# Another order for the beginning of a one-core kernel: wider modulation reads, first tokens earlier, gate weights in pairs

## The chip, the cores and the metric

The kernel runs on one core of a Trainium2 chip. The metric is the device time of one execution in microseconds (us); the median of three runs is compared. The engines go by the names of the profile: PE is TensorE's matmul (PEld its weight load), DVE is VectorE, ACT is ScalarE, POOL is GpSimd, and SP is SyncE, which issues most of the transfers (DMAs). Each engine works through its own queue in order, and an instruction that waits holds up all that stands behind it in that queue.

## What is computed

One layer of a flow-matching backbone for 2048 sample tokens and 128 prompt tokens of width 1024. Only the start of it matters here:

```python
def ada_mod(cvec, w, b):
    m = jnp.einsum('...d,de->...e', jax.nn.silu(cvec), w) + b
    return jnp.split(m, 3, axis=-1)
...
shift, scale, gate = ada_mod(c, w_ada[l], b_ada[l])
xn = rmsnorm(h, ln_g[l]) * (1.0 + scale[:, None, :]) + shift[:, None, :]
...
proj = jnp.einsum('btd,de->bte', xn, w_in)
qkv, beta, dec, z_a, u_b, v_b, z_b, x_c, z_c, gates = jnp.split(proj, points, axis=-1)
```

So nothing can be projected before shift and scale are known, and these need 2048 of the 3072 columns of `w_ada` (1024 rows, float32, 8.4 MB). The first projection that the kernel makes is `z_a` (512 columns, later put through SiLU and kept in memory as `sz`); then come `qkv` and the rest: a delta-rule mixer, a spatial gate, a Fourier mixer, merge gates and the output projection.

Each projection is made with three float16 matmuls, for activations and weights are both split into a high and a low part (`xh`, `xl`; `hi`, `lo`): hi·xh + hi·xl + lo·xh. Scales that are powers of two keep both in float16's range.

## The kernel before

**Queue order.** The Python program issues instructions engine by engine, and a planner then orders them by a simulated timeline and by priority: an instruction issued later may be put ahead of one issued earlier where the planner thinks that it can start sooner. `tc.high_priority()` raises the priority of what is issued inside it; `tc.issue_after(x)` keeps instructions behind `x`.

**Modulation (lines 396 to 430).** Eight blocks of 256 columns. Each is read in two chunks of four 128-row groups (`ast`, 512 KB each, eight buffers, line 403). In the blocks named in `AD` the second chunk is summed on DVE (`ada_sum`, lines 384 and 386: a column times a scalar for each of the two conditioning vectors, accumulated in `aacc`) and enters PE by one matmul for each vector (`sel`); everything else is a matmul with the two vectors as the stationary operand (line 411). The block's 2x256 result is copied from PSUM (`adr`, line 413) and transposed in two pieces (line 415). Ahead of block 4 (`XB`) the first 512 tokens are read (`xt`, 2 MB, line 393) and a few small parameters (`columns`, lines 360 to 367). After the last block, lines 420 to 430 make shift (`sh`), scale (`ms`) and a bound on the activations, from which their power-of-two scale `sx` is taken.

**Gate projection (lines 433 to 475).** The weights of `z_a` are four blocks of 128 columns (512 KB, two landing buffers `wst`), read by `read_w` (line 195) and converted by `converting`: squares with a sum (line 209), a power-of-two scale from it (`scales`, lines 180 to 188, with a small matmul and DVE operations), the high half on ACT (line 222), the low half on DVE (line 223). The loop over tiles of tokens (`TBS`: four of 512, then the 128 prompt tokens) makes, for each tile: four sums of squares on ACT (`jk`, line 451), `rsqrt` (lines 170 and 171, the power on POOL), a normalization on DVE (line 455); then for each of eight groups of 128 channels four transposes on PE (line 459), the modulation on DVE (`xm`, line 461, three buffers), the high half on ACT (`xh`, line 462) and the low half on POOL (`xl`, line 463); then for each of the four z blocks 24 matmuls (`gemm_T`, line 466), a sigmoid on ACT (line 468), a product on DVE (line 469) and the store (line 471). All matmuls stand in the helper `mm`, line 161.

**Weights further on.** `wlist` is the list of all later weight blocks. `fetch`, `weight_step` and `getw` read them two ahead and convert them in small steps; after the tile loop `ahead(2)` lets the first two qkv weights go. The read of `w_spatial` (line 649) stands in the program after the qkv projection.

Of the kernel before, what the change touches and what calls it, by code (L numbers as in the profile page):

```python
# [11 lines left out]
F16 = mybir.dt.float16  # L12
I32 = mybir.dt.int32
BF16 = mybir.dt.bfloat16
AF = mybir.ActivationFunctionType
# [16 lines left out]
QUOTA = 1.6  # L32
SCAN = 1.3
MT = 0.015
XB = 4
AD = (0, 2, 4, 6)
CQ = 545
FS = 4096.0
TBS = [(0, 512), (512, 512), (1024, 512), (1536, 512), (2048, 128)]
# [72 lines left out]
def hybrid_flow_kernel(ctx: ExitStack, tc: tile.TileContext, x_prompt, x_sample, state_delta, c, c_ctx, ln_g, w_ada,  # L112
# [47 lines left out]
    def mm(out, l, r, start=True, stop=True):  # L160
        PE.matmul(out, l, r, start=start, stop=stop)  # L161

    def mm3(out, l, r):
# [2 lines left out]
        mm(out, l[0], r[1], False, False)  # L166
        mm(out, l[1], r[0], False, True)

    def rsqrt(out, ss, mul, w):
        V.tensor_scalar(out, ss, mul, EPS, ALU.mult, ALU.add)  # L170
        G.tensor_tensor(out, out, mhalf.to_broadcast([P, w]), ALU.pow)  # L171
# [18 lines left out]
    def load_w(src, nkt, cols=P, hi=None, lo=None, tag="w", bufs=5):  # L190
        return convert(read_w(src, nkt, cols, tag), nkt, cols, hi, lo, tag, bufs)

    def read_w(src, nkt, cols=P, tag="w"):
        st = sb(wp, [P, nkt, cols], "wst" if cols == P else tag + "st", bufs=2 if cols == P else 1)
        SY.dma_start(st, src.rearrange("(k p) c -> p k c", p=P))
        return st

    def converting(w, st, nkt, cols=P, hi=None, lo=None, tag="w", bufs=5):

        wpool = bwp[0] if tag == "b" else wp  # L200
        if tag == "z":
            hi, lo = [sb(p0p, [P, nkt, cols], n_, F16, bufs=4) for n_ in ("zhi", "zlo")]
# [6 lines left out]
        A.activation(w.lo, st, AF.Square, accum_out=ss)  # L209
# [12 lines left out]
        A.activation(w.hi, st, AF.Copy, scale=s)  # L222
        V.scalar_tensor_tensor(w.lo, st, s, w.hi, ALU.mult, ALU.subtract)  # L223
# [27 lines left out]
    def xrows(t0, n):  # L251
        return xs_[t0:t0 + n, :] if t0 < NS else xp_[t0 - NS:t0 - NS + n, :]

    wlist = []
    for c0 in [C_ZA + g * P for g in range(4)]:
        wlist.append((w_in_[:, c0:c0 + P], KT, "z", 4))
# [122 lines left out]
    def ada_sum(acc, st, ks, fresh=True):  # L379

        for g in range(2):
            for i, k in enumerate(ks):
                if i == 0 and fresh:
                    V.tensor_scalar(acc[:, g, :], st[:, i, :], scT[:, k, g:g + 1], None, ALU.mult)
                else:
                    V.scalar_tensor_tensor(acc[:, g, :], st[:, i, :], scT[:, k, g:g + 1], acc[:, g, :], ALU.mult, ALU.add)
# [9 lines left out]
    for blk in range(8):  # L396
        if blk == XB:
            load_x(*TBS[0])
            columns()
        ps = bank(ps_d, [2, 256])  # L400
        for k0 in range(0, KT, 4):
            st = sb(p0p, [P, 4, 256], "ast", bufs=8)
            last_ada = SY.dma_start(st, w_ada_[k0 * P:(k0 + 4) * P, blk * 256:(blk + 1) * 256].rearrange("(k p) c -> p k c", p=P))
            if k0 and blk in AD:
                acc = sb(p0p, [P, 2, 256], "aacc")
                ada_sum(acc, st, range(k0, k0 + 4))
                for g in range(2):
                    mm(ps, sel[:, g, :], acc[:, g, :], False, g == 1)
                continue
            for k in range(4):  # L410
                mm(ps, scT[:, k0 + k, :], st[:, k, :], k0 + k == 0, k0 + k == KT - 1)
        adr = sb(p0p, [2, 256], "adr")
        V.tensor_copy(adr, ps)
        for k in range(2):
            PE.transpose(pa[:, blk * 2 + k, :], adr[:, k * P:(k + 1) * P], ident[:2, :2])
    ms = sb(cp, [P, KT, 2], "ms")
    sh = sb(cp, [P, KT, 2], "sh")
    with tc.high_priority():
# [12 lines left out]


    szD = dram("sz", [H, P, NTOK])
    with tc.issue_after(last_ada.ins):
        read_next()
        read_next()
        load_x(*TBS[1])
        zaw = getw(4)
        bdp = sb(wp, [P, KT, 32], "bdp", F16, bufs=1)
        bdw = load_w(w_in_[:, C_BD:C_BD + 16], KT, 16, hi=bdp[:, :, 0:16], lo=bdp[:, :, 16:32], tag="d")  # L440
    szlate = []
    for ti, (t0, tn) in enumerate(TBS):
        if t0 not in xts:
            load_x(t0, tn)
        g = 0 if t0 < NS else 1
        nt = tn // P
        xt = xts[t0]
        jk = sb(p0p, [P, D], "jk", F16, bufs=1)
        xss = sb(p0p, [P, nt], "xss")
        for j in range(nt):  # L450
            A.activation(jk, xt[:, j, :], AF.Square, accum_out=xss[:, j:j + 1])
        rs = sb(p0p, [P, nt], "rs")
        rsqrt(rs, xss, 1.0 / D, nt)
        for j in range(nt):
            V.tensor_scalar(xt[:, j, :], xt[:, j, :], rs[:, j:j + 1], None, ALU.mult)
        for k in range(KT):
            ps = bank(ps_d, [P, tn])
            for j in range(nt):
                PE.transpose(ps[:, j * P:(j + 1) * P], xt[:, j, k * P:(k + 1) * P], ident)
            t = sb(p0p, [P, tn], "xm", bufs=3)  # L460
            V.tensor_scalar(t, ps, ms[:, k, g:g + 1], sh[:, k, g:g + 1], ALU.mult, ALU.add)
            A.copy(xh[:, k, t0:t0 + tn], t)
            G.tensor_tensor(xl[:, k, t0:t0 + tn], t, xh[:, k, t0:t0 + tn], ALU.subtract)
        for g in range(4):
            ps = bank(ps_d if tn == P and g % 2 else ps_mm, [P, tn])
            gemm_T(ps, zaw[g], 0, xh[:, :, t0:t0 + tn], xl[:, :, t0:t0 + tn])
            sg = sb(ep, [P, tn], "sg", bufs=4)
            A.activation(sg, ps, AF.Sigmoid, scale=zaw[g].inv)
            V.scalar_tensor_tensor(sg, ps, zaw[g].inv, sg, ALU.mult, ALU.mult)
            if szlate:  # L470
                SY.dma_start(*szlate.pop())
            szlate.append((szD[g, :, t0:t0 + tn], sg))
    SY.dma_start(*szlate.pop())
    p0.close()
    ahead(2)


    def h3(ap):
# [170 lines left out]
    SY.dma_start(wsn, w_spatial[0].rearrange("g p q -> p g q"))  # L649
    pace.drain()  # L650
    a1.close()

# [909 lines left out]
```

## Time and profile before

| what | value |
|---|---|
| median of three runs | 2200.02 us (2197.28 to 2202.29) |
| the profiled execution's own time | 2200.34 us |
| its span, first to last instruction | 2198.2 us |
| mean granted PE clock | 0.993 |
| w_ada read up to the tile loop | 16 chunks of 512 KB |
| z weights | 4 blocks of 512 KB |

How such lines are read: in a timeline, a row has the start, the busy time (of several instructions that follow each other, with their count behind an x), the engine, the line of the program, the operation, output <- inputs with their shapes, and in brackets how long the engine stood idle before it and for what. A table of windows has one row for each stretch: its length, then the busy time of PE, PEld, DVE, ACT and POOL with the number of instructions, the granted PE clock, the mean busy share of the 16 DMA engines and the GB/s moved; one made for PE alone has only PE's column ahead of the clock. A row of a group has the shapes and the count, then total busy us and the mean ns of one, then the idle time before them by cause. The ends of PE's matmuls are modelled: 0.38 us is shown for one of 512 columns even where they follow each other every 0.22 us.

### The profile page before, as it was taken

To read this page: it belongs to the slowest core of one execution; us is meant where nothing else is said; L and a number is where in the kernel's file an instruction comes from. 1 tells how busy PE (TensorE), PEld (TensorE's weight loads), DVE (VectorE), ACT (ScalarE), POOL (GpSimd) and SP (SyncE) were. 2 spreads that over 40 slices of the span, in tenths; PEclk is the share of its full clock that TensorE was granted. 3 is DMA by queue.
4 is the path that set the end of the run, shared out by engine and by line. 5 is a ranking of instruction groups with operands and counts; after the bars stand their busy time and mean duration, and the time that the engine had idled before them with its cause. 6 is when DMAs were issued, how large, how long until landed. Compare 5 with 4: busy or idle time off the path is not lost. (4 is left out here: it accounts for less than half of the span.)

```text
span 2198.2 us, 42667 instructions
## 1 busy us (share of the span) xinstructions
PE 2125.9 (97%) x16234; PEld 1213.1 (55%) x16234; DVE 1311.2 (60%) x3140; ACT 1014.4 (46%) x2345; POOL 707.5 (32%) x862
## 2 busy tenths in 40 slices
PE   7999999999999999899899999999999999999998
PEld 3565444455555587777555555555654444444443
DVE  5746745469979698466665555765674544223454
ACT  3644644345466474355544445655553422222332
POOL 1421433223333322432322223344532221222543
PEclk9999999999999999999999999999999999999999
DMA  8324733167777662444655556776664544324542
GB/s 280 141 87 149 260 117 110 61 203 231 241 229 239 198 192 83 126 130 137 203 172 162 164 164 185 240 212 209 200 198 151 168 125 133 118 78 123 174 148 103
DMA packets 304568, 365.09 MB, mean 166 GB/s; under 512 B 39426, under 2 KB 215787, under 8 KB 302315
## 3 DMA queue, kind: packets, MB, share of 16 engines
q1 hardware_dynamic: 289226, 302.19, 45.6%
q0 software_dynamic: 12688, 51.27, 6.4%
q10 hardware_dynamic: 2448, 8.91, 1.0%
q8 instruction: 127, 2.08, 0.4%
q14 instruction: 79, 0.64, 0.1%
HBM read 234.67 MB, written 127.62 MB: 165 GB/s over the span
## 5 line engine op out<-in xcount | busy, mean ns | idle before, releaser
L161 PE MATMUL b<-xh,whi 128*128 128x512 f16 (+1 forms) x1920 | 652.8, 349 | 0.4 <-DVE mrow L1391 0.4
L161 PE MATMUL b<-xl,whi 128*128 128x512 f16 (+1 forms) x1920 | 652.9, 348 | 0.0
L161 PE MATMUL b<-xh,wlo 128*128 128x512 f16 (+1 forms) x1920 | 651.9, 348 | 0.5 <-DVE wlo L223 0.5
L161 PEld LDWEIGHTS <-whi 128*128 128x128 f16 x3904 | 358.8, 98 | 330.0 <-issue 9.4
L161 PEld LDWEIGHTS <-wlo 128*128 128x128 f16 x1952 | 191.7, 98 | 180.8 <-issue 5.0
L161 PE MATMUL b<-big,bhi 128*128 128x512 f16 (+1 forms) x960 | 250.6, 347 | 2.4 <-ACT big L1355 1.9
L1395 POOL TENSOR_TENSOR mrow<-mrow,sg 128x512 f32<-128x512 f32 (+1 forms) x80 | 91.8, 1148 | 293.9 <-DVE sg L1394 225.7
L161 PE MATMUL b<-big,blo 128*128 128x512 f16 (+1 forms) x480 | 162.9, 347 | 0.0
L1385 ACT ACTIVATE sg<-b,winv 128x512 f32<-128x512 f32 (+1 forms) x120 | 74.1, 618 | 174.5 <-PE b L161 173.7
L644 POOL TENSOR_TENSOR cy<-cy,raw 128x545 f32<-128x545 f32 (+1 forms) x48 | 74.9, 1586 | 184.2 <-ACT raw L643 184.2
L161 PEld LDWEIGHTS <-xh 128*128 128x128 f16 x1496 | 117.0, 98 | 28.1
L1394 DVE SCALAR_TENSOR_TENSOR sg<-b,binv,sg 128x512 f32<-128x512 f32 (+1 forms) x80 | 53.4, 667 | 126.1 <-PE b L161 119.3
L161 PEld LDWEIGHTS <-bhi 128*128 128x128 f16 x960 | 86.5, 98 | 73.6 <-issue 2.1
L175 DVE CAST wscb<-wss 128x1 bf16<-128x1 f32 x93 | 14.3, 154 | 148.5 <-ACT wlo L209 67.3
L864 POOL COPY T<-ES 32x256 f16<-32x256 f16 x68 | 30.5, 449 | 202.3 <-DMA ES<-ei 167.1
L161 PE MATMUL b<-whi,xh 128*128 128x128 f16 x544 | 92.9, 219 | 0.0
L161 PE MATMUL b<-wlo,xh 128*128 128x128 f16 x544 | 92.9, 219 | 0.0
L161 PE MATMUL b<-whi,xl 128*128 128x128 f16 x544 | 92.9, 219 | 0.0
L161 PE MATMUL b<-wohi,mh 128*128 128x512 f16 x240 | 90.9, 379 | 1.4 <-ACT mh L1462 1.4
L161 PE MATMUL b<-wohi,ml 128*128 128x512 f16 x240 | 90.8, 379 | 0.3 <-DVE mscb L175 0.3
L161 PE MATMUL b<-wolo,mh 128*128 128x512 f16 x240 | 90.9, 379 | 0.0
L209 ACT ACTIVATE wlo<-wst 128x1024 f16<-128x1024 f32 x52 | 55.0, 1057 | 77.5 <-DMA wst<-in_w_in_dram 74.1
(456 smaller groups left out, 4285.4 us busy)
## 6 DMA issues: line engine op xcount, KB each, us to landing
wst<-in_w_in_dram SPq DMA_DIRECT2D x60, 512.0 KB, 4.9
qkv<-cy POOLq DMA_DIRECT2D x12, 1089.0 KB, 5.4
st<-br SPq DMA_DIRECT2D x48, 256.0 KB, 4.6
mrow<-mrg SPq DMA_DIRECT2D x18, 512.0 KB, 3.6
mrow<-mrg SPq DMA_DIRECT2D x16, 576.0 KB
mrg<-mrow POOLq DMA_DIRECT2D x16, 576.0 KB, 3.6
dc<-dec SPq DMA_DIRECT2D x17, 512.0 KB, 4.7
kq<-qkv SPq DMA_DIRECT2D x34, 256.0 KB, 4.6
```

The costliest lines, as they stand in the source:

```text
L161: PE.matmul(out, l, r, start=start, stop=stop)
L175: V.tensor_copy(sb16, ss)
L209: A.activation(w.lo, st, AF.Square, accum_out=ss)
L644: G.tensor_tensor(y[:, c0:c1], y[:, c0:c1], raw[:, 1 + c0:1 + c1], ALU.mult)
L864: G.tensor_copy(T16[rows(a0, b), :, :, b], ES[0:32, :, 2 * a0 + b, :, wT])
L1385: A.activation(sg, ps, AF.Sigmoid, scale=gw.inv)
L1394: V.scalar_tensor_tensor(sg, ps, binv[:, 1:2], sg, ALU.mult, ALU.mult)
L1395: G.tensor_tensor(mr, mr, sg, ALU.add)
```

## The change

The modulation now goes over four blocks of 512 columns, each read in four chunks of two row groups (the chunks stay at 512 KB, and there are still 16 and eight buffers). `AD` names blocks 0 and 2; in these the first chunk goes to PE and the other three are summed on DVE, with two `sel` matmuls at the end of the block. A block's result is 2x512, copied at high priority, and transposed in four pieces. The parameters are read ahead of block 2. The first tokens are read in four parts of 512 KB between blocks 2 and 3, and block 3's chunks are issued after them.

The z weights are read right behind the last chunk as two pairs of 256 columns, each pair in two halves of four row groups, into `ast` buffers. One scale serves a pair. The conversion of the first pair and the whole transposing part of tile 0 are issued at high priority. In tile 0 the matmuls of two z blocks run in turn inside the loop over channel groups, over two PSUM banks. The second pair is converted behind tile 0's transposing part. The next tile's sums of squares and normalization (`next_x`) are issued after a tile's first z block (in tile 0 after the first pair).

A helper, `pinned`, keeps an instruction behind the 10 (or n) instructions of its engine that were issued before it; it stands on the squares of the second z pair, of the later tiles, and (with n = 3) of the first qkv weights. The reads of the second tile, of the small beta and decay weights, of the first qkv weights and of `w_spatial` are held behind the last z read. The conversion of the beta and decay weights moves behind tile 1, and `ahead(2)` into tile 2, whose loop and those after it also take weight steps.

```diff
-AD = (0, 2, 4, 6)
+AD = (0, 2)
...
+    def pinned(made, n=10):
+        ins = made.ins
+        before = (i for i in reversed(nc.cur_bb.bb.instructions) if i is not ins and i.engine == ins.engine)
+        for _, i in zip(range(n), before):
+            tc.add_manual_dep(ins, i.name, mybir.DependencyInfo(mybir.DependencyClass.NoSync, mybir.DependencyReason.DATA),
+                              reason="pinned")
+        return made
...
-        SY.dma_start(st, src.rearrange("(k p) c -> p k c", p=P))
+        with tc.issue_after(first[0]) if len(wread) < 6 and first else ExitStack():
+            SY.dma_start(st, src.rearrange("(k p) c -> p k c", p=P))
...
+    for blk in range(4):
+        if blk == 2:
             columns()
+        if blk == 3:
+            with tc.issue_after(last_ada.ins):
+                last_ada = load_first()
+            xt = normed(*TBS[0], 2, False)
+        ps = bank(ps_d, [2, 512])
+        acc = sb(p0p, [P, 2, 512], "aacc", bufs=1) if blk in AD else None
+        for k0 in range(0, KT, 2):
+            st = sb(p0p, [P, 2, 512], "ast", bufs=8)
+            with tc.issue_after(last_ada.ins) if blk == 3 else ExitStack():
+                last_ada = SY.dma_start(st, w_ada_[k0 * P:(k0 + 2) * P, blk * 512:(blk + 1) * 512].rearrange("(k p) c -> p k c", p=P))
+            if k0 and acc is not None:
+                ada_sum(acc, st, range(k0, k0 + 2), k0 == 2)
                 continue
+            for k in range(2):
                 mm(ps, scT[:, k0 + k, :], st[:, k, :], k0 + k == 0, k0 + k == KT - 1)
...
+    def read_z(pair):
+        sts = []
+        for h in range(2):
+            st = sb(p0p, [P, 4, 256], "ast", bufs=8)
+            first[:] = [SY.dma_start(st, w_in_[h * 512:(h + 1) * 512, C_ZA + pair * 256:C_ZA + (pair + 1) * 256].rearrange("(k p) c -> p k c", p=P)).ins]
+            sts.append(st)
+        return sts
...
+        for h, kk in enumerate(halves):
+            sq = A.activation(lo[:, kk, :], sts[h], AF.Square, accum_out=ss[:, h:h + 1])
+            if zaw:
+                pinned(sq)
+        V.tensor_add(ss[:, 2:3], ss[:, 0:1], ss[:, 1:2])
+        s, inv = scales(ss[:, 2:3], wp, "wsc")
...
+        convert_z(zst[1])
+        for g0 in (0, 2):
+            pss = [bank(ps_mm, [P, tn]) for _ in range(2)]
+            for k in range(KT):
+                x_ = [t_[:, k, t0:t0 + tn] for t_ in (xh, xl)]
+                for i in range(2):
+                    mm(pss[i], zaw[g0 + i].hi[:, k, :], x_[0], k == 0, False)
+                    mm(pss[i], zaw[g0 + i].lo[:, k, :], x_[0], False, False)
+                for i in range(2):
+                    mm(pss[i], zaw[g0 + i].hi[:, k, :], x_[1], False, k == KT - 1)
+            if g0 == 0:
+                xt = next_x(ti)
+            for i in range(2):
+                z_out(g0 + i, t0, tn, pss[i])
```

More of the change, by code (lines that the diff above doesn't have):

```diff
@@ L34 @@
 MT = 0.015
-XB = 4
-AD = (0, 2, 4, 6)
+AD = (0, 2)
 CQ = 545
@@ L252, in xrows @@
         return xs_[t0:t0 + n, :] if t0 < NS else xp_[t0 - NS:t0 - NS + n, :]
-    wlist = []
-    for c0 in [C_ZA + g * P for g in range(4)]:
-        wlist.append((w_in_[:, c0:c0 + P], KT, "z", 4))
+    wlist, first = [], []
+    wlist.extend([None] * 4)
     for c0 in ([C_QKV + i * P for i in range(12)] + [C_V + g * P for g in range(4)]
@@ L394, in load_x, with load_first @@
         xts[t0] = xt
-    for blk in range(8):
-        if blk == XB:
-            load_x(*TBS[0])
-            columns()
[L400 to L408, printed above, removed]
+    def load_first():
+        xt = sb(p0p, [P, 4, D], "xt")
+        for j in range(4):
+            d_ = SY.dma_start(xt[:, j, :], xrows(j * P, P))
+        xts[0] = xt
+        return d_
@@ new lines, in normed @@
+    def normed(t0, tn, step, pin=True):
+        xt = xts[t0]
+        jk = sb(p0p, [P, D], "jk", F16, bufs=1)
+        for j0 in range(0, tn // P, step):
+            js = range(j0, min(j0 + step, tn // P))
+            xss = sb(p0p, [P, len(js)], "xss")
+            for j in js:
+                sq = A.activation(jk, xt[:, j, :], AF.Square, accum_out=xss[:, j - j0:j - j0 + 1])
+                if pin:
+                    pinned(sq)
+            rs = sb(p0p, [P, len(js)], "rs")
+            rsqrt(rs, xss, 1.0 / D, len(js))
+            for j in js:
+                V.tensor_scalar(xt[:, j, :], xt[:, j, :], rs[:, j - j0:j - j0 + 1], None, ALU.mult)
+        return xt
@@ L416, in hybrid_flow_kernel @@
+        with tc.high_priority():
+            V.tensor_copy(adr, ps)
+        for k in range(4):
+            PE.transpose(pa[:, blk * 4 + k, :], adr[:, k * P:(k + 1) * P], ident[:2, :2])
     ms = sb(cp, [P, KT, 2], "ms")
@@ L442, in hybrid_flow_kernel @@
+    with tc.high_priority():
+        convert_z(zst[0])
     for ti, (t0, tn) in enumerate(TBS):
-        if t0 not in xts:
-            load_x(t0, tn)
-        g = 0 if t0 < NS else 1
+        m = 0 if t0 < NS else 1
         nt = tn // P
[L447 to L472, printed above, removed]
+        with tc.high_priority() if ti == 0 else ExitStack():
+            for k in range(KT):
+                ps = bank(ps_d, [P, tn])
+                for j in range(nt):
+                    PE.transpose(ps[:, j * P:(j + 1) * P], xt[:, j, k * P:(k + 1) * P], ident)
+                t = sb(p0p, [P, tn], "xm", bufs=3)
+                V.tensor_scalar(t, ps, ms[:, k, m:m + 1], sh[:, k, m:m + 1], ALU.mult, ALU.add)
+                A.copy(xh[:, k, t0:t0 + tn], t)
+                G.tensor_tensor(xl[:, k, t0:t0 + tn], t, xh[:, k, t0:t0 + tn], ALU.subtract)
@@ new lines, in hybrid_flow_kernel @@
+        if ti:
+            for g in range(4):
+                ps = bank(ps_d if tn == P and g % 2 else ps_mm, [P, tn])
+                gemm_T(ps, zaw[g], 0, xh[:, :, t0:t0 + tn], xl[:, :, t0:t0 + tn])
+                z_out(g, t0, tn, ps)
+                if ti == 2 and g == 0:
+                    ahead(2)
+                if ti > 1:
+                    weight_step()
+                if g == 0:
+                    xt = next_x(ti)
+            if ti == 1:
+                bdw = convert(bdst, KT, 16, hi=bdp[:, :, 0:16], lo=bdp[:, :, 16:32], tag="d")
+            continue
@@ L473, in hybrid_flow_kernel @@
     SY.dma_start(*szlate.pop())
     p0.close()
-    ahead(2)
     def h3(ap):
@@ L648, in hybrid_flow_kernel @@
     wsn = sb(ep, [P, WB], "st", bufs=3).rearrange("p (g q) -> p g q", g=4)
-    SY.dma_start(wsn, w_spatial[0].rearrange("g p q -> p g q"))
+    with tc.issue_after(first[0]):
+        SY.dma_start(wsn, w_spatial[0].rearrange("g p q -> p g q"))
     pace.drain()
```

57 lines of the change are left out of this document (45 added, 12 removed).

## The prediction

> **What bounds the kernel now.** The page comes first, then the table of windows cut at the stages of the beginning.
>
> ```profile
> span 2198.2 us, 42667 instructions
> PE 2125.9 (97%) x16234; PEld 1213.1 (55%) x16234; DVE 1311.2 (60%) x3140; ACT 1014.4 (46%) x2345; POOL 707.5 (32%) x862
> 0.00:48.60 48.60, 33.97 (x152) 14.00 (x153) 22.58 (x73) 11.69 (x23) 1.79 (x10) 0.98 0.92 297
> 48.60:63.10 14.50, 12.43 (x63) 6.65 (x62) 13.12 (x19) 10.68 (x21) 13.04 (x9) 0.94 0.63 217
> 63.10:148.60 85.50, 85.50 (x447) 44.67 (x446) 51.50 (x98) 44.97 (x76) 33.24 (x30) 1.00 0.35 115
> 148.60:264.00 115.40, 115.40 (x926) 62.61 (x925) 75.54 (x86) 61.32 (x88) 35.71 (x32) 1.00 0.52 171
> ```
>
> TensorE (PE) sets the end, and from 63.1 to 264 us it has no gap. So the change can win only ahead of 63.1 us: what counts is how early the gapless stretch would start if the z stage had no holes. That stage ends at 148.64:
>
> ```profile
> 71.96 0.38 PE L161 MATMUL b<-xh,zhi 128*128 128x512 f16 x1
> 77.14 1.25 PE L459 MATMUL b<-cst,xt 128*128 128x128 f32 x10
> 78.23 0.38 PE L161 MATMUL b<-xh,zhi 128*128 128x512 f16 x1
> 148.64 0.22 PE L161 MATMUL b<-xh,zhi 128*128 128x128 f16 x1
> ```
>
> Between the first two rows lie 24 matmuls in 5.18 us, 0.216 us each; ten transposes take 1.09 us, 0.109 each. One 512-token tile is 96 matmuls and 32 transposes, 20.7 + 3.5 = 24.2 us. Four tiles are 96.9; the last tile's transposes and the scale matmuls add 0.8 (estimate). 148.64 - 97.7 gives a **virtual start at 50.9 us**. The prediction is this number for the changed kernel; behind it everything hangs on the qkv matmuls and shifts as a whole.
>
> Ahead of it the queues bound: the DMA share is 0.92 up to 48.6.
>
> ```profile
> 9.00:15.00 6.00, 6.00 (x20) 1.83 (x19) 2.99 (x8) 0.00 (x0) 0.00 (x0) 1.00 1.10 349
> 41.00:42.00 1.00, 0.17 (x1) 0.00 (x0) 0.00 (x0) 0.97 (x2) 0.00 (x0) 1.00 1.02 418
> 39.06 1.06 ACT L209 ACTIVATE zlo<-wst 128x1024 f16<-128x1024 f32 x1 [11.11 <-DMA wst<-in_w_in_dram]
> 40.82 1.06 ACT L209 ACTIVATE zlo<-wst 128x1024 f16<-128x1024 f32 x1 [0.60 <-DMA wst<-in_w_in_dram]
> 23.72 0.50 SPq L649 DMA_DIRECT2D st<-in_w_spatial_dram  x1
> SPq L403 <- DMA xt<-in_x_sample_dram: 4.7, 1, 4.7
> ```
>
> The first window moves w_ada, 256 columns wide (1 KB pieces), at 349 GB/s; the second moves token rows (4 KB pieces) at 418. Two z weights (512 KB each, 512 B pieces) land 1.76 us apart: 298 GB/s. The first landed at 39.06, so the last w_ada chunk ahead of it landed at about 37.3.
>
> **The change, part by part.**
>
> *Reading.* 8.39 MB of w_ada now come in 2 KB pieces. No row has these. A cost per piece plus a cost per byte through 349 (1 KB) and 418 (4 KB) gives 390 GB/s: 24.0 us become 21.5, -2.5. The bounds are 349 (nothing) and 418 (-3.9). The w_spatial read (256 KB, 0.9 us at 298), which stood among the last w_ada reads, waits for the z weights now: -0.9. Against it stands the issue order. The SP row shows an issue waiting for a transfer eight places earlier, so about eight are outstanding at once. Now five tiny parameter reads stand behind eight w_ada chunks, with no 2 MB token read ahead of them as cover, and hold slots: I put the bubble at +0.5 (bounds 0 and 1.5, one chunk's transfer). The last chunk lands at 37.3 - 2.9 = 34.4.
> The Trainium skill, "DMA: Bandwidth & Descriptors", section Specifications, has transfers at line rate from 512 B up. By it, wider pieces bring nothing and the 2.5 us fall away; the rates here rise from 298 over 349 to 418, and speak against it.
>
> *Summing.* VectorE now takes three chunks of four in two blocks, 24 operations of 512 columns, for 32 of 256. By the rows below (473 and 350 ns at 256 columns, 744 at 512) that is some 17 us for 14. It is done before the token read (5 us of transfer) has passed; without that cover it would hold the landing buffers.
>
> *From the last chunk to the first modulated tile.*
>
> ```profile
> 38.41 1.46 PE L161 MATMUL b<-ast,scT 128*2 128x256 f32 x6
> 40.57 0.59 PE L161 MATMUL b<-ast,scT 128*2 128x256 f32 x2
> 42.00 0.16 DVE L175 CAST wscb<-wss 128x1 bf16<-128x1 f32 x1 [1.60 <-ACT zlo L209]
> 42.07 0.73 DVE L413 COPY adr<-b 2x256 f32<-2x256 f32 x2
> 43.65 0.17 DVE L420 TENSOR_TENSOR sh<-b,pc 128x16 f32<-128x16 f32 x1 [0.84 <-PE b L415]
> 46.22 0.80 DVE L461 TENSOR_SCALAR xm<-b,ms,sh 128x512 f32<-128x512 f32 x1
> ```
>
> From 37.3 to 46.22 are 8.9 us: PE ended its sums at 41.16, behind a partial sum and transposes, and the copy then stood behind a cast that waited for a z weight. Now the last block is all on PE: two matmuls of 512 columns (0.9, twice the pace of these rows), one copy at high priority (0.7), four small transposes (0.4), the 2.57 us of 43.65 to 46.22, semaphores 0.3: 4.9. First modulation at 34.4 + 4.9 = **39.3**.
>
> *First z pair.*
>
> ```profile
> L463 POOL TENSOR_TENSOR xl<-xm,xh 128x512 f16<-128x512 f32 x32 | 41.6, 1318 | 52.4 <-ACT xh L462 52.4
> L461 DVE TENSOR_SCALAR xm<-b,ms,sh 128x512 f32<-128x512 f32 x32 | 25.0, 803 | 6.3 <-PE b L459 5.6 <-POOL xl L463 0.6
> L462 ACT CAST xh<-xm 128x512 f16<-128x512 f32 x32 | 19.3, 614 | 17.5 <-DVE xm L461 17.1
> L451 ACT ACTIVATE jk<-xt 128x1024 f16<-128x1024 f32 x17 | 17.9, 1052 | 20.3 <-DMA xt<-in_x_sample_dram 18.9 <-DMA xt<-in_x_prompt_dram 1.2
> L222 ACT ACTIVATE zhi<-wst,wsc 128x1024 f16<-128x1024 f32 x4 | 4.6, 1148 | 6.5 <-DVE wsc L186 6.5
> L223 DVE SCALAR_TENSOR_TENSOR zlo<-wst,wsc,zhi 128x1024 f16<-128x1024 f32 x4 | 5.1, 1276 | 0.3 <-ACT zhi L222 0.3
> L386 DVE SCALAR_TENSOR_TENSOR aacc<-ast,scT,aacc 128x256 f32<-128x256 f32 x24 | 10.0, 473 | 0.0
> L384 DVE TENSOR_SCALAR aacc<-ast,scT 128x256 f32<-128x256 f32 x8 | 2.5, 350 | 10.5 <-DMA ast<-in_w_ada_dram 10.5
> L469 DVE SCALAR_TENSOR_TENSOR sg<-b,winv,sg 128x512 f32<-128x512 f32 x16 | 11.7, 744 | 13.6 <-ACT sg L468 13.6
> L455 DVE TENSOR_SCALAR xt<-xt,rs 128x1024 f32<-128x1024 f32 x17 | 16.3, 1009 | 2.1 <-POOL rs L171 1.9
> 47.00:48.00 1.00, 0.92 (x5) 0.50 0.00 0
> 50.00:51.00 1.00, 0.81 (x4) 0.79 0.06 8
> 48.65 6.62 POOL L463 TENSOR_TENSOR xl<-xm,xh 128x512 f16<-128x512 f32 x4 [19.23 <-ACT xh L462]
> 48.65 2.14 POOL L463 TENSOR_TENSOR xl<-xm,xh 128x512 f16<-128x512 f32 x1 [19.23 <-ACT xh L462]
> 53.94 0.59 PE L161 MATMUL b<-xh,zhi 128*128 128x512 f16 x2
> 62.73 0.55 PE L459 MATMUL b<-cst,xt 128*128 128x128 f32 x3 [0.94 <-DVE wsc L186]
> ```
>
> Its halves (1 KB pieces, 1.5 us each) land at 35.9 and 37.4. On ScalarE the second half's squares (1.05 and 0.2 for the accumulator) and the two small bound squares (0.8) end at 39.2; scale chain 1.3, first hi half 1.15: z matmuls from **41.7**. Pair one is 48 matmuls (10.4) and 20 transposes still to do (2.2); the granted clock was 0.50 for 3.7 us at this place (rows 47 and 50) after a gap like the one that remains, +1.85. It ends at 56.1. GpSimd's eight subtractions (xl), from 42.2 at 1.5 (near the 1.65 of the row of four), end at 54.2: beside it. Work done is 13.85, so the virtual start would be 42.2.
>
> *Second z pair.* Its squares are pinned behind ten ScalarE instructions, so behind the tile's last cast. That cast needs the fifth xl (three xm buffers): 42.2 + 7.5 + 0.8 + 0.6 = 51.1. Two squares 2.5, chain 1.4, hi 1.15, lo 1.28: the first lo at 57.4, the first hi at 56.2. PE is free at 56.1: a **new wait** of 0 to 1.3 (hi matmuls go in front, or don't); I take 0.7. It replaces the old waits on z weights three and four (row 62.73). Queued behind the pinned squares are the next tile's own.
>
> *Second tile.* Those four squares start after the second hi half, at 57.3, and take 5.0, two sigmoids 1.3, rsqrt 1.4, the four normalizations 3.0 (0.74 each with GpSimd idle, in the trace; 1.01 by the mean): 68.0. Transpose, modulation and cast: first xh at 69.7; xl at 1.32 each end at 80.3. PE has pair two done at 67.2. If matmuls of two z blocks fill in for each other, as row 53.94 shows them doing (two hi in a row), it loses 69.7 - 67.2 - 1.3 (three banks of transposes) = 1.2; if the first block runs alone, 80.7 instead of 67.2 + 3.5 + 5.2 = 75.9: 4.8. I take 2.2, nearer to the row. Later tiles have a whole tile's PE time (24.2) for the same chain (some 22 from the pinned squares to the last xl): nothing.
>
> *Moved, and costed at nothing.* The z reads use w_ada buffers whose sums are over by 28. The second tokens follow them (2 MB, 5.0 at 418 after the last z half at 40.4) and land near 46; they are needed at 57. The small beta and decay weights are converted after the second tile and first used after the last. w_spatial is used later still. Two qkv weights are read and converted in steps during the third and fourth tile: eight of the twelve weight steps, per tile some 2.4 us of ScalarE, which has 24.2 a tile and needs 12.6 without them (eight casts 4.9, squares 5.0, four sigmoids of 0.68). If that cover went, PE would wait for one read and conversion chain, 9 us, ahead of qkv.
>
> **Sum.** 42.2 + 0.7 + 2.2 = 45.1 for 50.9: **-5.8 us**. The profiled execution took 2200.34 (span 2198.2 and 2.1 around it), 0.3 above the median 2200.02. Forecast **2194.6**.
>
> **Rivals.**
> 1. *No new waits*: squares fit earlier, both waits vanish: 50.9 - 42.2 = 8.7, 2191.7. Against it: the pins.
> 2. *Pieces bring no rate* (the skill's rule): landing 2.5 later, gain 3.3: 2197.1. Against it: the three rates.
> 3. *Second tile's first block alone*: gain 5.8 - 2.6 = 3.2: 2197.2. For it: xl is the slow step.
> 4. *The order isn't as written*: the scheduler moves reads on its own (w_spatial, from line 649, stood between w_ada reads), so the tail is as long as before: 2200.3.
> 5. *GpSimd becomes the bound*, slower. Both tiles' chains now run one behind the other, and hold 5 + 8 = 13 subtractions in series. With p each and no filling, the virtual start is 42.2 + 5p + 1.4, + 18.6 to the next first xh, + 8p + 0.4, - 32.9 of work = 29.7 + 13p. It decides from p = 1.63; at 1.97 it is slower by 0.2%; at 2.14 (the single row of the first) 57.5, so 2206.9. For it: 1.65 in tile 0 beside lo conversions; against it: the mean 1.32. The Trainium skill, "GPSIMD Engine Reference", section 1. Specifications, has GpSimd share its SBUF interfaces with VectorE, with contention from operations with two SBUF inputs, as the lo conversion is; by it the price rises where both run.
>
> **How the numbers follow.** Forecast 0.47, rival 1 0.10, 2 0.14, 3 0.12, 4 0.07, 5 0.10. About 0.2%, 4.4 us, can be told from no change. Faster: 0.42 of the forecast and rival 1, 0.52; within: 0.05, rivals 2 to 4, 0.38; slower: 0.10. The range leaves out rival 5 and rival 1's end with 418 GB/s (below 2191): 2191.0 to 2201.0.
>
> **What would show it.** The last modulation sum by 36 and the first xm by 40 (reading right); the w_ada window near 390 GB/s; z matmuls from 42; a PE wait near 56 on zlo and near 67 on xt or xm; gapless until the small tile, which starts near 143. Wrong if xm comes after 43, if xl takes over 1.6, or if PE gaps open behind 264.

## The result and the profile after

The changed kernel is **slower**: 2211.35 us (median of six runs, 2208.35 to 2214.69) against 2198.65 for the kernel before (six runs on the same chip), a ratio of 1.0056 [1.0043, 1.0068]. The forecast was 2194.6, and its range ended at 2201.0.

The page of the profiled execution, whose own time was 2211.37 us, begins so:

```profile
span 2209.4 us, 42520 instructions
PE 2127.9 (96%) x16168; PEld 1206.1 (55%) x16168; DVE 1312.5 (59%) x3119; ACT 1015.2 (46%) x2345; POOL 706.1 (32%) x863
```

TensorE has the work of before, in a span that is 11.2 us longer. To find the place, the windows behind the beginning come first, of after and then of before; both start at a point where the gapless stretch runs.

```profile
160.00:275.00 115.00, 115.00 (x924) 62.58 (x924) 82.58 (x107) 65.28 (x95) 34.32 (x34) 1.00 0.55 189
275.00:2209.40 1934.40, 1877.57 (x14658) 1084.01 (x14656) 1149.06 (x2862) 885.93 (x2141) 626.37 (x783) 0.99 0.53 164
```

```profile
264.00:2198.20 1934.20, 1878.61 (x14653) 1085.19 (x14651) 1148.45 (x2867) 885.72 (x2141) 623.68 (x782) 0.99 0.53 164
```

From 275 us after and from 264 us before, both need 1934 us to the end. All of the loss lies ahead of that, and it is there when the small tile (the 128 prompt tokens) begins, 160.32 for 148.64 (the last row of the next but one fence). Two spans divide the beginning: up to the first modulated tile (`xm`, 46.22 before), and from there to the small tile (102.4 us before).

The **front** comes first: three windows (length, busy PE, PEld, DVE, ACT, POOL, clock, DMA share, GB/s), then rows of the timelines of PE, DVE and ACT, of after.

```profile
15.00:19.50 4.50, 4.50 (x7) 0.72 (x6) 1.74 (x3) 0.00 (x0) 0.00 (x0) 1.00 0.81 258
26.00:33.00 7.00, 3.06 (x13) 0.99 (x12) 6.39 (x12) 4.60 (x8) 2.47 (x1) 0.73 1.04 399
29.00:33.00 4.00, 1.56 (x3) 0.21 (x3) 3.39 (x7) 1.92 (x4) 2.47 (x1) 0.52 1.05 390
36.77 1.06 ACT L486 ACTIVATE zlo<-ast 128x1024 f16<-128x1024 f32 x1 [5.72 <-DMA ast<-in_w_in_dram]
38.27 1.06 ACT L486 ACTIVATE zlo<-ast 128x1024 f16<-128x1024 f32 x1 [0.36 <-DMA ast<-in_w_in_dram]
31.46 1.87 PE L160 MATMUL b<-aacc,sel 128*2 128x512 f32 x2 [2.44 <-DVE aacc L394]
33.12 3.32 PE L160 MATMUL b<-ast,scT 128*2 128x512 f32 x4
36.28 1.02 PE L160 MATMUL b<-aacc,sel 128*2 128x512 f32 x2
37.49 1.88 PE L160 MATMUL b<-ast,scT 128*2 128x512 f32 x4
39.55 1.88 PE L160 MATMUL b<-ast,scT 128*2 128x512 f32 x4
41.73 1.88 PE L160 MATMUL b<-ast,scT 128*2 128x512 f32 x4
43.54 0.66 PE L538 MATMUL b<-cst,xt 128*128 128x128 f32 x4
44.13 0.41 PE L453 MATMUL b<-cst,adr 2*128 2x2 f32 x4
44.57 0.68 DVE L451 COPY adr<-b 2x512 f32<-2x512 f32 x1 [4.77 <-PE b L453]
48.81 1.53 DVE L540 TENSOR_SCALAR xm<-b,ms,sh 128x512 f32<-128x512 f32 x2
```

The reading is early: the first z half lands at 36.77 and the second 1.5 us behind it, so the last chunk of `w_ada` had landed about 1.5 us ahead of the first, at 35.3 (an estimate; 37.3 before). But the sums end at 43.6, for 41.16 before. Block 3's four chunks stand on PE behind the first of block 2's two closing matmuls (`sel`), with the second between them, and the first chunk runs at half clock. The first `xm` comes at 48.81, 2.6 us later than before.

The **z stage** loses more. PE's timeline of after, with ACT's and DVE's rows that it waits for:

```profile
60.52 1.05 ACT L486 ACTIVATE zlo<-ast 128x1024 f16<-128x1024 f32 x1
66.82 1.03 PE L160 MATMUL b<-xh,zhi 128*128 128x512 f16 x2 [2.17 <-ACT zhi L494]
96.04 0.69 ACT L516 ACTIVATE sg<-b,winv 128x512 f32<-128x512 f32 x1 [6.17 <-PE b L160]
96.63 1.05 ACT L418 ACTIVATE jk<-xt 128x1024 f16<-128x1024 f32 x1
103.57 2.74 DVE L424 TENSOR_SCALAR xt<-xt,rs 128x1024 f32<-128x1024 f32 x4 [1.19 <-POOL rs L179]
104.42 2.49 PE L538 MATMUL b<-cst,xt 128*128 128x128 f32 x12 [0.22 <-PE b L160]
107.80 0.66 PE L538 MATMUL b<-cst,xt 128*128 128x128 f32 x4 [0.56 <-DVE xm L540]
132.56 2.49 PE L538 MATMUL b<-cst,xt 128*128 128x128 f32 x12 [1.46 <-issue]
135.88 0.66 PE L538 MATMUL b<-cst,xt 128*128 128x128 f32 x4 [0.83 <-DVE xm L540]
160.32 0.28 PE L160 MATMUL b<-xh,zhi 128*128 128x128 f16 x2
```

Three holes are seen: 2.17 us at the second z pair, and one ahead of the third tile (near 104) and of the fourth (near 132). The rows around 100 us say how the last two arise: ScalarE stands idle for 6.17 us for the last matmul of the second tile's first z block, does its sigmoid, and only then takes up the next tile's squares, which had been free to run; so the normalization is late and PE's transposes trickle, 12 in 2.49 us. From first `xm` to small tile it is 160.32 - 48.81 = 111.5 us, 9.1 more than before.

### The profile page after: what moved, and what is told of

The parts are those of the page before. It is cut to its first block, busy times and chain, and to the rows that moved or that the text cites. A ratio compares the mean times of both kernels' runs of the same rounds, so it can differ in the third digit from the quotient of the medians.

```text
span 2209.4 us, 42520 instructions
## 1 busy us (share of the span) xinstructions
PE 2127.9 (96%) x16168; PEld 1206.1 (55%) x16168; DVE 1312.5 (59%) x3119; ACT 1015.2 (46%) x2345; POOL 706.1 (32%) x863
## 5 line engine op out<-in xcount | busy, mean ns | idle before, releaser
L232 DVE SCALAR_TENSOR_TENSOR wlo<-wst,wsc,whi 128x1024 f16<-128x1024 f32 x52 | 70.7, 1361 | 29.4 <-ACT whi L231 29.2
```

## The experiments

In each text of what was expected, A and B (or the names there) are the theories at issue in that run. Ratios are to the kernel before on the same chip, with the 95% interval. In the table, "xm" is the start of the first modulated tile, "small" that of the small tile's first matmul in the profiled execution, and "z stage" their difference. The whole front lies up to 1.7 us earlier or later from one profiled execution to the other with the same code in it (after has 48.81, the latest; e1, e5, e6, e8 and e12 have 47.16 to 47.68), so the last column and the ratio carry the comparison. The medians come from several chips: the kernel before has 2199.22 beside e1 to e4, 2197.11 beside e5 to e8 and 2198.43 beside e9 to e12.

| kernel | median, us | ratio | xm | small | z stage |
|---|---|---|---|---|---|
| before | 2198.65 | 1 | 46.22 | 148.64 | 102.4 |
| after | 2211.35 | 1.0056 [1.0043, 1.0068] | 48.81 | 160.32 | 111.5 |
| e1 no pins | 2197.76 | 0.9999 [0.9988, 1.0009] | 47.55 | 149.84 | 102.3 |
| e2 modulation alone | 2195.38 | 0.9991 [0.9982, 1.0] | 46.20 | 149.15 | 103.0 |
| e3 z part alone | 2208.54 | 1.0043 [1.0029, 1.0057] | 45.88 | 158.10 | 112.2 |
| e4 `sel` late | 2210.26 | 1.0053 [1.004, 1.0066] | 47.88 | 158.42 | 110.5 |
| e5 z pin off | 2204.80 | 1.0033 [1.0019, 1.0046] | 47.33 | 154.41 | 107.1 |
| e6 later tiles' pins off | 2207.43 | 1.0049 [1.0033, 1.0066] | 47.36 | 156.71 | 109.4 |
| e7 no pins, tokens last | 2191.88 | 0.9982 [0.9971, 0.9992] | 41.74 | 146.22 | 104.5 |
| e8 squares ahead of sigmoid | 2202.09 | 1.0018 [1.0008, 1.0028] | 47.68 | 152.12 | 104.4 |
| e9 before, tokens last | 2200.86 | 1.001 [1.0002, 1.0019] | 42.12 | 151.50 | 109.4 |
| e10 e2, tokens last | 2194.31 | 0.9982 [0.9973, 0.9991] | 42.38 | 144.81 | 102.4 |
| e11 e12, tokens last | 2190.94 | 0.9971 [0.996, 0.9982] | 41.95 | 143.19 | 101.2 |
| e12 e5 and e8 together | 2198.58 | 1.0 [0.9991, 1.0008] | 47.16 | 147.65 | 100.5 |

**e1: all pins off.** Everything else of the change stays.

```diff
     def pinned(made, n=10):
+        return made
```

> The changed kernel with no instruction pinned. Theory A (the pins make the late preparation of z pair two and of tiles 2 to 4, and PE runs dry at each): PE's idle time between 52 and 160 us falls from 7.2 to under 2 us and the small tile's matmuls start 6 to 8 us earlier than 160.3, so about 2204 us. Theory B (GpSimd's subtractions, now in series, are the bound): the idle time stays and the time is within 2 us of the changed kernel's 2211.

The loss is gone, and so is any gain: 2197.76 us. The small tile comes 10.5 us earlier than after, more than the 6 to 8 of theory A, and the z stage is as long as before. The pins cost what the change loses; they alone don't explain why nothing is won.

**e2 and e3: one half of the change each.** e2 is the kernel before with the new blocks, chunks, parameters and token reads (and the read of `w_spatial` held behind them). e3 is the other half: modulation of before, with the z pairs, the pins and the new loop over tiles.

e2 against before, cut to its core:

```diff
-AD = (0, 2, 4, 6)
+AD = (0, 2)
...
-    for blk in range(8):
+    for blk in range(4):
...
```

and e3 against after:

```diff
-AD = (0, 2)
+XB = 4
+AD = (0, 2, 4, 6)
...
-    for blk in range(4):
+    for blk in range(8):
...
```

> The kernel before with only the modulation and its reads changed (blocks of 512, first tokens before the last block, w_spatial's read held behind the last modulation read); the tile loop and the z weights are those of before. Theory A (the front loses: the last, 512 wide block lies wholly on PE, behind a sum that waits for VectorE, with a cold clock): first modulation near 48.8 instead of 46.2, about 2201 to 2202 us. Theory B (the front gains what its reads gain, all loss is in the z stage): first modulation by 44, 2196 us or less.

> The kernel before with only the z part and the tile loop changed (pairs, halves, pins, order); the modulation is that of before, first tokens read ahead of block 4 of 8. Theory A: first modulation near 46, the z stage 8 us longer than before, about 2206 to 2208 us. Theory B (all loss is in the front): 2199 us or less.

The z part alone makes most of the loss (1.0043), with the z stage as long as after the whole change. The new modulation alone neither loses nor wins much: its first `xm` stands at 46.20, as before, so neither theory's place for it (48.8, or 44) came true. Its sums, in PE's timeline of e2, are those of after, 1.2 us earlier:

```profile
30.23 1.87 PE L160 MATMUL b<-aacc,sel 128*2 128x512 f32 x2 [2.37 <-DVE aacc L385]
31.89 3.25 PE L160 MATMUL b<-ast,scT 128*2 128x512 f32 x4
```

The two halves don't simply add up: 0.9991 and 1.0043 for 1.0056 together. From the end of the sums to `xm` e2 needs 4.1 us (42.07 to 46.20), after 5.2.

**e4: is it the wait for DVE?** Block 2's `sel` matmuls go behind block 3's matmuls on PE, with a buffer of their own for the copy, so that nothing of block 3 stands behind the wait of 2.44 us.

```diff
+        if blk == 2:
+            held = (blk, ps, acc, True)
+            continue
+        if blk == 3:
+            close(*held)
+        close(blk, ps, acc, False)
```

(`close` holds the `sel` matmuls, the copy and the transposes as they were.)

> The changed kernel with block 2's two sel matmuls kept behind block 3's matmuls on PE (its 2x512 result in a buffer of its own); nothing else. Theory A (PE stood 2.4 us for VectorE's sum ahead of landed data, and ran the next 7 matmuls at half clock for it): PE's last sum ends near 40 instead of 43.6, first modulation near 45.5 instead of 48.8, about 3 us off the changed kernel's time. Theory B (it is the amount of f32 matmul work in the last block alone, 1.9 us a chunk against 1.35 a landing): the last sum ends at 42.5 or later, under 1 us.

PE's timeline of e4:

```profile
32.07 3.26 PE L160 MATMUL b<-ast,scT 128*2 128x512 f32 x4 [3.82 <-DMA ast<-in_w_ada_dram]
41.48 1.88 PE L160 MATMUL b<-aacc,sel 128*2 128x512 f32 x4
```

The wait for DVE is gone; PE now stands 3.82 us for the chunk itself, and the sums still end at 43.4 (41.9 to 43.6 where block 3 is as in the change: e12, after). So the wait is not the cause. What e4 keeps is the amount, four chunks and two closing matmuls, all behind the token read, and the half clock of the first chunk (3.26 for 1.88); no run takes that half clock away alone.

**e7: the tokens last.** That is tested by moving them: the first tokens are read behind block 3's chunks (pins off).

```diff
-        if blk == 3:
-            with tc.issue_after(last_ada.ins):
-                last_ada = load_first()
-            xt = normed(*TBS[0], 2, False)
...
+    with tc.issue_after(last_ada.ins):
+        last_ada = load_first()
+    xt = normed(*TBS[0], 2, False)
```

> The changed kernel with no pins, and the first tokens read after the last modulation block instead of ahead of it, in front of the z weights. If the front is held by PE's backlog of f32 matmuls behind the last landings (theory A), the 2 MB of tokens cover it: last modulation sum near 38, first modulation at 41 to 42 instead of 47.6 (by then the tokens are normalized at about 40), small tile 5 us earlier than 149.8, about 2193 us. If the front is held by the amount of data alone (theory E), tokens last make the first modulation no earlier than 46: within 1.5 us of the kernel without pins, 2198.

A window of e7 (columns as above), and two rows of its PE:

```profile
26.00:33.00 7.00, 7.00 (x20) 1.51 (x19) 4.67 (x8) 1.96 (x3) 0.00 (x0) 1.00 1.04 407
29.58 3.60 PE L160 MATMUL b<-ast,scT 128*2 128x512 f32 x8
33.01 1.88 PE L160 MATMUL b<-aacc,sel 128*2 128x512 f32 x4
```

PE is busy without a gap and at full clock in the window in which it was at 0.73 after the change, and the sums end at 34.9 instead of 43.6. Two things are in that: the last chunk lands earlier, and less is left to sum behind it. The first token part is taken up at 30.84, so by 1.3 us for its 512 KB (at the window's 407 GB/s) the last chunk had landed at about 29.6, and the sums end 5.3 us behind it, for 8.3 after; these 5.3 us pass beside the token read. The first `xm` is at 41.74, 5.8 us earlier than in e1 and not 8.7, for now the tokens' normalization (its last part from 37.84 to 39.2) comes late. This is the first version that clearly beats the kernel before, 0.9982.

**e5, e6, e8: which pin?** e5 takes the pin off the squares of the second z pair, e6 off the squares of the later tiles. e8 keeps both, but issues the next tile's squares ahead of the first block's sigmoid in the tiles behind tile 0, so that a pinned square no longer has that sigmoid ahead of it.

```diff
-            if zaw:
-                pinned(sq)
```

```diff
-    def normed(t0, tn, step, pin=True):
+    def normed(t0, tn, step, pin=False):
```

```diff
+                if g == 0:
+                    xt = next_x(ti)
                 z_out(g, t0, tn, ps)
...
-                if g == 0:
-                    xt = next_x(ti)
```

> The changed kernel with the pin on the second z pair's squares alone taken off. Theory C (each pin costs its own hole: 2.2 us of waiting and some 1.6 of half clock at pair two; 1.3 and 2.9 at the third and fourth tile): the wait on zhi near 65 is gone, the waits near 104 and 131 stay, the small tile starts 3 to 5 us earlier than 160.3, about 2207 us. Theory D (one pin carries all, since what it holds back queues up behind it): 9 us earlier, 2200 us or less.

> The changed kernel with the pins on the later tiles' squares taken off, that of the second z pair kept. Theory C: the waits near 104 and 131 go, the wait on zhi near 65 stays, small tile 4 to 5 us earlier, about 2207 us. Theory D with the z pin as the one that carries all: under 1.5 us, 2210 us.

> The changed kernel with all pins, but the next tile's squares issued ahead of the first z block's sigmoid in tiles 1 to 3, so that the pins no longer put them behind it. Theory F (the sigmoid, which waits for PE to end that block, is what makes the later tiles late): squares of the third tile start near 90 instead of 96.6, the waits near 104 and 131 go, about 3 to 4 us off the changed kernel, 2207 us. Rival (the pins behind the casts suffice to make them late): under 1 us.

With e5 the wait of 2.17 us on `zhi` is gone, and the z stage is 4.4 us shorter. With e8 it is 7.1 shorter, more than the 3 to 4 expected, and PE has no wait left behind 78 us. ACT and PE of e8, for the third tile:

```profile
88.67 1.05 ACT L418 ACTIVATE jk<-xt 128x1024 f16<-128x1024 f32 x1
94.93 1.33 ACT L516 ACTIVATE sg<-b,winv 128x512 f32<-128x512 f32 x2 [1.57 <-PE b L160]
97.75 1.47 PE L538 MATMUL b<-cst,xt 128*128 128x128 f32 x12
```

The squares run in the time in which ScalarE was idle, and the 12 transposes take 1.47 us in place of 2.49. That difference stood in the timeline of after inside a row of busy time: a wait inside a row of several instructions is not shown as idle.

e6, which takes those pins away altogether, gains only 2.2 us of z stage, where 4 to 5 were expected. A window and two rows of PE show why:

```profile
60.00:78.00 18.00, 12.08 (x59) 6.49 (x58) 15.33 (x23) 14.24 (x25) 10.35 (x10) 0.82 0.52 200
71.49 0.93 PE L538 MATMUL b<-cst,xt 128*128 128x128 f32 x4 [1.72 <-DVE wsc L195]
74.43 1.46 PE L160 MATMUL b<-xh,zhi 128*128 128x512 f16 x3 [2.02 <-ACT zhi L494]
```

Freed, the second tile's squares and normalization are put ahead of the second z pair's squares and scale, which are still pinned, and PE waits for that instead. The hole needs the one pin that is left: e1, without any, has no such wait.

**e9 to e12: what adds up.** e12 has the edits of e5 and e8. e11 has these and e7's move of the tokens, which makes it the whole change with its two holes closed and the tokens last. e9 moves the tokens last in the kernel before, and e10 in e2; in both the first tile is then also normalized in twos, and in e9 read in four parts (the excerpts leave that out).

e9 against before:

```diff
         if blk == XB:
-            load_x(*TBS[0])
             columns()
...
+    with tc.issue_after(last_ada.ins):
+        last_ada = load_first()
+    xt0 = normed(*TBS[0], 2)
```

and e10 against e2:

```diff
-        if blk == 3:
-            with tc.issue_after(last_ada.ins):
-                last_ada = load_first()
...
+    with tc.issue_after(last_ada.ins):
+        last_ada = load_first()
+    xt0 = normed(*TBS[0], 2)
```

> The kernel before with one thing moved: the first 512 tokens are read behind the last modulation chunk instead of ahead of block 4, in four parts and normalized in twos; modulation in 256 wide blocks, z weights and tile loop as before. Theory A (PE's f32 sums run behind the last landings, and tokens can cover them): last sum near 37 instead of 41, first modulation at 42 to 43 instead of 46.2, about 3 us faster than before (ratio 0.9985). Theory E (data alone): first modulation at 46 or later, same as before or slower, since the tokens' squares and normalization now come last.

> As the kernel with the changed modulation alone, with the first tokens behind the last modulation chunk. If wider pieces add anything to the order: landings 2.5 us earlier than with 256 columns, first modulation 1 to 2 us earlier than in the kernel before with tokens last, ratio about 0.998. If the order is all: the same as that kernel.

> The changed kernel with both mends (next tile's squares ahead of the first sigmoid, z pair's pin off), tokens where the change has them. If the two holes add up: ratio 1.0056 less 0.0038 and 0.0023, about 0.9995, like the kernel with no pins. If one takes over from the other: 1.0015 or more.

> The changed kernel with tokens last, next tile's squares ahead of the first sigmoid with their pins kept, and the z pair's pin off. Theory G (a pin behind the tile's casts alone costs nothing): as the kernel with no pins and tokens last, ratio 0.998 to 0.9985, no PE wait over 1 us behind 60. Rival (any pin costs): 3 us or more behind that kernel.

The two holes of the pins are nearly independent: e5 takes 0.0023 off the ratio and e8 0.0038, and 1.0056 less both is 0.9995; e12 has 1.0. Its z stage of 100.5 us is 1.9 shorter than that of before: so much the new z part wins in this profile once the holes are closed. With the tokens last the front is 5.2 us earlier than in e12, on the same chip, and e11, 2190.94 us, beats both kernels and has no PE wait over 1 us behind 60. Its 0.9971 and the 0.9982 of e7 and e10 overlap in their intervals, so it isn't shown to be faster than these.

e9 missed: its sums end at 35.9 and its `xm` comes at 42.12, but the time rises to 2200.86. PE's rows in e9:

```profile
60.03 2.10 PE L474 MATMUL b<-cst,xt 128*128 128x128 f32 x12 [0.56 <-DVE xm L476]
66.28 0.39 PE L161 MATMUL b<-xh,zhi 128*128 128x512 f16 x1 [3.80 <-ACT zhi L222]
```

The gain at the front becomes a wait of 3.8 us for the conversion of the later z weights. e10, with the same two landing buffers for them, has no such wait. SP's reads, of e9 and then of e10, differ there:

```profile
47.59 0.37 SPq L393 DMA_DIRECT2D xt<-in_x_sample_dram  x1
48.16 3.75 SPq L195 DMA_DIRECT2D wst<-in_w_in_dram  x2
```

```profile
46.18 3.58 SPq L194 DMA_DIRECT2D wst<-in_w_in_dram  x2
52.88 0.37 SPq L392 DMA_DIRECT2D xt<-in_x_sample_dram  x1
```

In e9 the third tile's tokens (2 MB) are read ahead of the third and fourth z weight, in e10 behind them; and in e9 ScalarE takes up that tile's squares at 55.70, ahead of those of the two weights at 57.93 and 60.58. That is the likely cause, but an e9 with that order alone was not tried.

e10 missed in one point: its time is as expected (0.998), but its first `xm`, 42.38, is not 1 to 2 us earlier than e9's 42.12. With the tokens last the wider pieces brought nothing at that place, though e10's first token part is taken up 1.4 us earlier (31.66 for 33.06); what holds `xm` there was not tried.

## Why the prediction was wrong

**The base held.** The text said that behind the gapless stretch everything shifts as a whole: 1934.4 us after and 1934.2 before, 11.7 us of delay at the small tile and 11.2 in the span. How close these two are is partly luck: from the small tile to the end, the fourteen profiled executions took 2042.6 (e10) to 2052.8 us (e11, whose profiled execution took 2198.0 for a median of 2190.94). The forecast had the small tile at 148.6 - 5.8 = 142.8. The error of 17.5 us at that place is 9.5 in the front (`xm` at 39.3 against 48.81) and 8.0 in the z stage (103.5 forecast, 111.5 measured). The text's own sign of being wrong, `xm` after 43, was met. (Its 2194.6 takes the gain off the profiled execution's 2200.34; off the median, 2200.02, it would be 2194.2.)

**Reading: right.** Pieces of 2 KB moved at 390 GB/s, as in the window 29 to 33, the interpolated value. The bubble was at the upper end of its bounds: between 15.0 and 19.5 the queues moved 258 GB/s, and 4.5 us at 258 for 390 is 1.5 us, for 0.5 taken. That gives 37.3 - 2.5 - 0.9 + 1.5 = 35.4, near the 35.3 read above, for 34.4 forecast. SP's timeline of after fits the cause that the text named, tiny parameter reads each waiting for a chunk to land (no run moved them); no chunk is issued for seven us:

```profile
7.65 0.38 SPq L368 DMA_DIRECT2D prm<-in_ln_g_dram  x1
13.33 0.32 SPq L372 DMA_DIRECT2D prm<-in_b_ada_dram  x1
14.78 3.46 SPq L440 DMA_DIRECT2D ast<-in_w_ada_dram  x4
```

Rival 2 falls with it: the Trainium skill, "DMA: Bandwidth & Descriptors", section Specifications, has line rate from 512 B up, and here the same volume went at 349 in pieces of 1 KB and at 390 in pieces of 2 KB.

**Summing: its cover was wrong.** VectorE was to be done with block 2 before the token read had passed. It ended at 32.07, while the last token part was taken up at 29.89: hence PE's wait of 2.44 us. By e4 that wait is not what made the front late.

**From last chunk to first modulated tile: the first step that failed**, by its size. The text put "two matmuls of 512 columns (0.9, twice the pace of these rows)" behind the last chunk; the sums ended 8.3 us behind it (35.3 to 43.6). That is 7.4 of the 9.5 us; 0.9 is the landing and 1.2 the way from the sums to `xm`, 5.2 for 4.0. About 1.3 of the 9.5 belongs to this one execution, by the other `xm` with the same front. The groups up to 160 us, of after and of before, show the unit:

```profile
L160 PE MATMUL b<-ast,scT 128*2 128x512 f32 x40 | 24.3, 752 | 5.4 <-DMA ast<-in_w_ada_dram 5.4
```

```profile
L161 PE MATMUL b<-ast,scT 128*2 128x256 f32 x96 | 25.2, 413 | 5.9 <-DMA ast<-in_w_ada_dram 5.9
```

The program makes 20 such calls after (blocks 0 and 2 two each, 1 and 3 eight each) and 48 before (four blocks of four, four of eight). Each float32 matmul is thus two records. A chunk of two calls takes 1.88 us of PE at full clock, the double of what was taken, and 3.3 at half clock, while one lands each 1.35 us (512 KB at 390). So PE falls behind with every chunk that it sums itself, and the last block is all its own. That the backlog, and not the wait, holds the front is shown by the pair: e4 removes the wait and the sums end where they did; in e7 PE sums the same chunks while DVE still sums block 2, a backlog of 5.3 us passes beside the token read, and `xm` comes 5.8 us earlier than in e1. How the 8.3 us divide between amount and half clock is read from rows alone (at half clock the first chunk took 1.4 more, the first closing matmul 0.9 more). What the text called cover, the token read between blocks 2 and 3, is time in which PE has nothing to sum and after which all of its last work begins. Block 2's two closing matmuls, which the text did not cost, came on top: 1.02 at full clock and 1.87 at half. A smaller part is read from the rows alone and was not tried: behind the sums, four of tile 0's transposes (43.54), issued at high priority, stood on PE ahead of block 2's (44.13), for which the copy of block 3's result waited until 44.57, 0.9 us after the sums ended; and four more stood ahead of block 3's own. In e2, where they have no such priority, they came behind, and `xm` followed the sums in 4.1 us for 5.2.

**Second z pair: right place, wrong size.** The wait on the second pair's hi half was foreseen at 56, "0 to 1.3", 0.7 taken. It came at 66.82 with 2.17 us, and at half clock behind it (two matmuls in 1.03). The rows say what the text missed, though no run tried it alone: it let the scale chain run beside PE's first pair, but the chain has a small matmul of its own (`wscb`, ready at 63.1), which PE reached only at 64.48, behind that pair; the chain's remaining steps and the first hi half came after it. e5, which takes the pin off, removes the wait and shortens the z stage by 4.4 us.

**Second tile: too dear.** Of the 2.2 us put in for it, next to nothing came: between 79 and 84 us PE was idle for 0.16. There the second pair was itself late; but e12, where it isn't, has no PE wait over 0.4 us between 50 and 160 either.

**Later tiles: "nothing" was the second step that failed**, and the dearer one. The text compared lengths, PE's 24.2 us a tile with some 22 for the chain from the pinned squares to the last `xl`. It took the chain to begin with the tile. It begins with the first block's sigmoid: the ten instructions that the squares are pinned behind include it, and it waits for the last matmul of the first z block of the tile before, until 96.04 where the third tile is prepared. Then the chain has only the time of the other three blocks. The text named the sigmoids as work for the second tile and did not ask what they wait for. e8 moves the same squares ahead of that sigmoid and wins 7.1 us of the z stage. Without its waits (0.7 and 2.2) the forecast z stage was 100.6 us; e12, with both holes closed, has 100.5. So the rest of the stage was counted right in sum, and the waits were what failed: 2.9 forecast, 11.0 measured between after and e12, with the half clock and the trickle that come with them.

**The rivals.** None had this mechanism. Rival 5, the only slower one (0.10), was so for another reason, GpSimd's subtractions in series, deciding from 1.63 us each:

```profile
L542 POOL TENSOR_TENSOR xl<-xm,xh 128x512 f16<-128x512 f32 x32 | 38.0, 1218 | 36.3 <-ACT xh L541 36.3
```

They took 1.22 us in the mean, less than the 1.32 of before, and tile 0's eight took 10.81 together, 1.35 each. By the Trainium skill, "GPSIMD Engine Reference", section 1. Specifications, GpSimd shares its SBUF interfaces with VectorE and contends with VectorE's instructions that have two SBUF inputs. The trace agrees for single ones: tile 0's first subtraction, which starts at 51.24 beside the lo conversion, took 2.02 us for a median of 1.16, and the second lo conversion took 2.17 for 1.27 of the first. Rival 1 (no new waits, 2191.7) is nearest to what e11 reached, 2190.94; that is luck, for e11 has a mended order and a later token read.

## What to carry to other kernels

A pin behind the last n instructions of an engine takes over every wait among them; before it is costed at nothing, ask of each what releases it, and put the work that is free to run ahead of the one that waits for another engine. Where a read stream is summed by two engines, the slower one's share must not come last: let the other transfers follow the last summed chunk, so that the backlog drains beside them. Then look at the order of the later reads again, for in e9 the gain of the front was lost behind it. And count a matmul's cost from records per call, not from one record.

## What the runs showed of the hardware

A float32 matmul of 512 columns is two records of 0.45 us (eight in 3.60 us in e7), 0.83 each at half clock (four in 3.32).

The granted clock fell where PE had gaps: after PE had stood for 2.44 us, with 1.56 us of work in the 4 us from 29 to 33, it was 0.52 there; in e7, where the same stretch has no gap, it was 1.00. The chunk behind that wait took 1.4 us more than the others (3.32 for 1.88). Near the start of a span the shown clock can't be relied on: between 15.0 and 19.5 it reads 1.00, while eight such records from 13.36 on took 6.35 us, 0.79 each, the pace of half clock.

The queues moved 298 GB/s in pieces of 512 B, 349 in 1 KB and 418 in 4 KB (before), and 390 in 2 KB (after).

Twelve transposes that take 1.47 us when their input is ready were shown as one row of 2.49 us where it trickled in. Compare a group's duration with its own best before taking it for work.
